# Stick-breaking attention summed by parts, in a hand-made pipeline of pieces

## The chip, the cores and the metric

The kernel runs on one core of a Trainium2 chip. The metric is the device time of one execution in microseconds (us), as the median of several runs; lower is better. The core has five engines with instruction queues of their own: TensorE (PE; its weight loads are listed as PEld), VectorE (DVE), ScalarE (ACT), GpSimd (POOL) and SyncE (SP), which here only issues DMAs. Each engine takes its own instructions strictly in the order in which they were laid down.

## The reference, cut to what matters

Two transformer layers on a sequence of 2048 positions and 1024 channels. The change touches one of three mixers of the second layer, the stick-breaking attention, which has 4 heads of 64 channels:

```
z       = q k^T / 8                       (128 queries at a time, all keys up to them)
log_1mb = where(mask, log_sigmoid(-z), 0)              (mask: key s < query t)
suffix  = cumsum(log_1mb, reverse) - log_1mb
a       = where(mask, exp(log_sigmoid(z) + suffix), 0)
out     = a v,  then an RMS norm for each head
```

Written without logarithms: let G[s] be the product of (1 - beta[j]) over all j from s to the end of the row. Then a[s] = G[s+1] - G[s], and out = sum over s of a[s] v[s]. The other mixers of this layer are a differential attention (4 heads, "diff") and a small windowed mean ("pool mixer").

## The kernel before, in words

Block 1, the whole first layer, takes the first part of the time and the feed-forward network the last; between them lies the attention stage (`block2`), from about 960 to 1975 us. It runs six units one after the other, in the order stick, diff, diff, stick, diff, diff. A stick unit holds two heads (r = 0 and 1). Each unit starts with four GEMM blocks of 512 positions (`unit_gemm`, its inner function `gemm`), which make keys, values and queries as pairs of float16 numbers (a high part and the remainder, the "low part"), and then goes over 16 rows of 128 queries; row i has (i + 1) * 128 keys. Up to four GEMM blocks are emitted ahead of the rows that use them. Tiles of keys, values and queries come from the pool U of 11 buffers, of which a unit takes 8.

A stick row (`stick`) is worked for each head in pieces of at most 1024 keys (PIECE), from the last keys to the first:

- `scores` makes z in PSUM for the whole row (lines 832, 833, 835), on TensorE.
- ScalarE writes sigmoid(-z) = 1 - beta into the tile g (line 973); one more column behind it holds 1.0 (a GpSimd memset, line 968) or the value carried from the piece before (VectorE copies, lines 970 and 980).
- VectorE's scan multiplies from right to left (line 975): g now holds G.
- GpSimd subtracts neighbours, A[s] = G[s+1] - G[s] (line 981).
- `parts` splits A into float16 halves: ScalarE casts the high part (line 845) and an engine that the caller names, VectorE for stick, subtracts to get the low part (line 846). A DMA transposes both (line 848).
- `spread` multiplies the transposed pieces with the values and adds them into PSUM (lines 869 and 870), when all pieces of the row and head are there.

A diff row uses `parts` and `spread` too, with GpSimd for the low part. The tiles g and A, and the two of a diff row, come from one pool E of 10 buffers (a piece of up to 512 keys takes one buffer for both).

The order of instructions on each engine is not that of the Python code: a list scheduler replays the program on a model of the chip and emits what is ready, earlier code first. So TensorE's GEMM matmuls of the next unit fill gaps between the pieces of the one that runs.

Of the kernel before, what the change touches and what calls it, by code (L numbers as in the profile page):

```python
# [7 lines left out]
F32 = mybir.dt.float32  # L8
# [31 lines left out]
PON = 2  # L40
EN = 10
UN = 11
LAST_B = 2
UNITS = (0, 2, 3, 1, 4, 5)
MIX_ROWS = (0, 2)
# [21 lines left out]
class Kernel:  # L67
# [638 lines left out]
    def block2(self):  # L706
        self.y2d = self.y_scratch("y2d")
        with ExitStack() as c2:
            self.ep = self.pool("E", EN, ctx=c2)
# [4 lines left out]
            self.sm = self.pool("asm", 4, ctx=c2)  # L714
            self.pg = self.pool("pg", PGN, PSUM, ctx=c2)
            self.sc = self.pool("sc", SCN, PSUM, ctx=c2)
# [4 lines left out]
            units = [units[j] for j in UNITS]  # L721
            self.turn = self.turn2 = 0
            self.later = []
            for u, (kind, k, *w) in enumerate(units):
                ops, gemm = self.unit_gemm(w)
                done = 0
# [20 lines left out]

    def etile(self):
        return self.ep.tile([128, PIECE + 8], F32, tag="e", name="e")

# [30 lines left out]

    def unit_gemm(self, cols):

# [3 lines left out]
        ks = [self.up.tile([128, S], F16, tag="u", name=f"k{r}") for r in range(2)]  # L787
        vs = [self.up.tile([128, NT // 2, 2, 128], F16, tag="u", name="v") for _ in range(2)]
        qs = []

        def gemm(b):
# [10 lines left out]
            ps = self.gemm_ct(wv, b)  # L802
            vt = self.one.tile([128, 2, 512], F16, tag="vt", name="vt")
            nc.scalar.copy(vt[:, 0], ps)
            nc.vector.tensor_tensor(vt[:, 1], ps, vt[:, 0], ALU.subtract)
            for x in range(2):
                nc.sync.dma_start_transpose(vs[b // 2][:, b % 2 * 4:b % 2 * 4 + 4, x], vt[:, x])
            ps = self.gemm_ct(wq, b)
# [8 lines left out]

        return (qs, ks, vs), gemm

    def scores(self, ops, r, i, strict):  # L820

        nc = self.nc
        qs, ks, _ = ops
        q = qs[i // 4][:, r, :, i % 4 * 128:(i % 4 + 1) * 128]
        W = (i + 1) * 128
        out = []
        for p in range(0, W, 512):
# [23 lines left out]
    def etiles(self, n):  # L851

        if self.last_rows:
            self.turn += 1
            e = self.tp.tile([128, 2, PIECE], F32, tag=("th", "tl")[self.turn % 2], name="e")
            return e[:, 0], e[:, 1]
        if n <= PIECE // 2:
            e = self.etile()
            return e[:, 0:PIECE // 2 + 8], e[:, PIECE // 2 + 8:]
        return self.etile(), self.etile()  # L860

    def spread(self, pieces, ops, cols, po):

# [3 lines left out]
        for x, (t, j, k) in enumerate(todo):  # L867
            v = ops[2][k // 8][:, k % 8, :, cols]
            nc.tensor.matmul(po, t[:, 0, j], v, start=x == 0, stop=False)  # L869
            nc.tensor.matmul(po[:, 0], t[:, 1, j], v[:, 0], start=False, stop=x == len(todo) - 1)  # L870

# [8 lines left out]
    def diff(self, ops, k, b):  # L880
# [3 lines left out]
        for c in range(4):  # L884
            po = self.po.tile([128, 2, 128], F32, tag="po", name="po")
            i = b * 4 + c
            W = (i + 1) * 128
            E = [(self.etiles(n), n) for n in (min(PIECE, W - p) for p in range(0, W, PIECE))]
            ss = self.sm.tile([128, 2, 4], F32, tag="ss", name="ss")
# [24 lines left out]
            for x, ((e1, e2), n) in enumerate(E):  # L914
                nc.vector.scalar_tensor_tensor(e1[:, 0:n], e2[:, 0:n], cf, e1[:, 0:n], ALU.mult, ALU.add)
                eng = nc.gpsimd if (i + x) % 4 < LO_POOL else nc.vector
                pieces.append((self.parts(e1, e2, n, eng), x * (PIECE // 128), n // 128))
            self.spread(pieces, ops, slice(0, 128), po)
# [32 lines left out]
    def stick(self, ops, k, b):  # L951

        nc = self.nc
        o8 = self.m.tile([128, 4, 2, 128], F32, tag="o4", name="o8")
        for c in range(4):
            po = self.po.tile([128, 2, 128], F32, tag="po", name="po")
            i = b * 4 + c
            W = (i + 1) * 128  # L960
            for r in range(2):
                sc = self.scores(ops, r, i, True)
                pieces, carry = [], None
                for p0 in reversed(range(0, W, PIECE)):
                    n = min(PIECE, W - p0)
# [5 lines left out]
                    for ps, p, w in sc:  # L971
                        if p0 <= p < p0 + PIECE:
                            nc.scalar.activation(g[:, p - p0:p - p0 + w], ps[:, 0:w], AF.Sigmoid, scale=-1.0)
                    rev = g[:, 0:n + 1][:, ::-1]
# [3 lines left out]
                    if p0:  # L978
                        carry = self.sm.tile([128, 1], F32, tag="carry", name="carry")
                        nc.vector.tensor_copy(carry, g[:, 0:1])  # L980
# [3 lines left out]
            nc.vector.tensor_copy(o8[:, c], po)  # L984
            yield

        o4 = self.summed(o8)

        def done():
            self.head_norm(o4, 64)  # L990
            self.finish(o4, k, b, self.col("sg"))

        self.later.append((LAST_DELAY if self.last_unit else DELAY, done))

# [356 lines left out]
```

## Time and profile before

| what | value |
|---|---|
| median of 3 runs | 3413.29 us (3409.84 to 3413.64) |
| profiled execution, its own time | 3417.88 us |
| span of the profiled execution | 3416.1 us |
| TensorE busy over the span | 3110.3 us (91%) |
| VectorE busy | 2274.2 us (67%) |
| ScalarE busy | 1217.8 us (36%) |
| GpSimd busy | 1357.9 us (40%) |
| mean granted TensorE clock | 0.969 of full speed |

The span is what the rows of the trace add up to; the time of the execution is 1.8 us longer, and lies 4.6 us above the median of the three runs. Busy shares are means over stages with different limits, so the stages have to be read apart.

### The profile page before, as it was taken

How to read it: one execution, taken by the hardware profiler on the slowest of the kernel's cores; microseconds unless marked ns; L12 is line 12 of the kernel's file. 1: busy time of each engine (PE TensorE's matmuls, PEld its weight loads, DVE VectorE, ACT ScalarE, POOL GpSimd, SP SyncE). 2: the span in 40 equal slices, each digit the busy share in tenths (PEclk: the TensorE clock that was granted, in tenths of full speed). 3: DMA queues.
4: the chain of work that ended last, by engine and by line, in shares of the span. 5: the costliest groups of instructions: out<-in, count | busy, mean ns of one | idle time of the engine just before them, and what ended most of it. 6: DMA issues, size and time to landing. Idle time of an engine off the chain costs nothing. (4 is left out here: it accounts for less than half of the span.)

```text
span 3416.1 us, 46957 instructions
## 1 busy us (share of the span) xinstructions
PE 3110.3 (91%) x17736; PEld 1576.9 (46%) x17736; DVE 2274.2 (67%) x3661; ACT 1217.8 (36%) x2291; POOL 1357.9 (40%) x1197
## 2 busy tenths in 40 slices
PE   8999998999988789958779898899999999989998
PEld 4454454785434445534335443344444444434443
DVE  6986979525638888879895744465655656754427
ACT  5223232322124466744564632233222332311103
POOL 5344344403335544565562511332322233244324
PEclk9999999999999899989999999899999999999999
DMA  5102021216756666646645788422222222453324
GB/s 189 38 17 47 13 50 44 58 44 176 179 140 125 125 127 134 134 96 125 127 91 106 154 214 195 117 69 80 80 84 68 74 90 81 161 190 134 110 98 168
DMA packets 597891, 371.85 MB, mean 109 GB/s; under 512 B 500640, under 2 KB 541344, under 8 KB 596640
## 3 DMA queue, kind: packets, MB, share of 16 engines
q1 hardware_dynamic: 590144, 348.22, 40.2%
q10 hardware_dynamic: 7520, 20.63, 1.8%
q8 instruction: 139, 2.28, 0.3%
q14 instruction: 88, 0.72, 0.1%
HBM read 162.70 MB, written 82.31 MB: 72 GB/s over the span
## 5 line engine op out<-in xcount | busy, mean ns | idle before, releaser
L144 PE MATMUL pg<-th,w 128*128 128x512 f16 x1344 | 520.2, 388 | 34.1 <-DVE r L592 11.6
L146 PE MATMUL pg<-th,w 128*128 128x512 f16 x1344 | 518.4, 386 | 7.2 <-POOL w L123 4.0
L145 PE MATMUL pg<-tl,w 128*128 128x512 f16 x1344 | 520.3, 387 | 0.7 <-DVE tl L183 0.7
L869 PE MATMUL po<-v,e 128*128 128x128 f16 (+1 forms) x1088 | 161.4, 252 | 98.6 <-DMA e<-e 85.3
L981 POOL TENSOR_TENSOR e<-e 128x128 f32<-128x128 f32 (+7 forms) x96 | 165.8, 1729 | 196.4 <-DVE e L975 145.8
L845 ACT CAST e<-e 128x1024 f16<-128x1024 f32 (+7 forms) x192 | 150.2, 794 | 224.6 <-POOL e L968 107.0
L846 POOL TENSOR_TENSOR e<-e 128x1024 f16<-128x1024 f32 (+4 forms) x96 | 157.5, 1655 | 180.3 <-ACT e L845 168.2
L145 PEld LDWEIGHTS <-w 128*128 128x128 f16 x1344 | 133.8, 100 | 175.3 <-issue 35.4
L144 PEld LDWEIGHTS <-w 128*128 128x128 f16 x1344 | 133.9, 100 | 171.6 <-issue 16.0
L146 PEld LDWEIGHTS <-w 128*128 128x128 f16 x1344 | 133.7, 100 | 165.8 <-issue 13.5
L975 DVE TENSOR_TENSOR_SCAN e<-e,few 128x129 f32<-128x129 f32 (+7 forms) x96 | 181.5, 1894 | 39.8 <-POOL e L968 31.0
L1075 POOL TENSOR_TENSOR w<-ws,w 128x1024 f16<-128x1024 f32 x20 | 48.6, 2431 | 393.0 <-ACT w L1074 393.0
L1107 PEld LDWEIGHTS <-w 128*128 128x128 f16 x1232 | 121.1, 98 | 172.9 <-issue 32.9
L832 PE MATMUL sc<-k,q 128*128 128x512 f16 (+2 forms) x480 | 174.1, 364 | 28.9 <-DVE e L895 23.7
L1106 PEld LDWEIGHTS <-w 128*128 128x128 f16 x1232 | 121.1, 98 | 165.5 <-ACT w L1074 18.7
L467 DVE SCALAR_TENSOR_TENSOR acc<-h,cols,acc 128x512 f32<-128x512 f32 x240 | 193.4, 826 | 2.4
L900 ACT ACTIVATE e<-e,nm 128x1024 f32<-128x1024 f32 (+4 forms) x192 | 171.1, 892 | 59.7 <-DVE e L895 39.1
L1108 PEld LDWEIGHTS <-w 128*128 128x128 f16 x1232 | 121.1, 98 | 150.0 <-issue 3.5
L833 PE MATMUL sc<-k,q 128*128 128x512 f16 (+2 forms) x480 | 171.7, 365 | 0.0
L869 PEld LDWEIGHTS <-e 128*128 128x128 f16 x1088 | 104.7, 101 | 126.5 <-issue 61.7
L123 POOL TENSOR_TENSOR w<-ws,w 128x1024 f16<-128x1024 f32 x52 | 120.2, 2313 | 96.1 <-ACT w L122 94.2
L870 PE MATMUL po<-v,e 128*128 128x64 f16 (+1 forms) x1088 | 155.3, 211 | 0.0
(318 smaller groups left out, 8018.1 us busy)
## 6 DMA issues: line engine op xcount, KB each, us to landing
mid<-md SPq DMA_DIRECT2D x88, 448.0 KB, 4.1
ws<-in_w SPq DMA_DIRECT2D x48, 512.0 KB, 3.9
md<-mid SPq DMA_DIRECT2D x44, 512.0 KB, 3.4
md<-mid SPq DMA_DIRECT2D x22, 768.0 KB, 5.0
q<-qn SPq DMA_DIRECT2D x96, 128.0 KB, 2.4
ws<-in_wg SPq DMA_DIRECT2D x22, 512.0 KB, 3.5
ws<-in_wu SPq DMA_DIRECT2D x22, 512.0 KB, 4.1
ws<-in_wd SPq DMA_DIRECT2D x22, 512.0 KB, 4.1
```

The costliest lines, as they stand in the source:

```text
L144: nc.tensor.matmul(ps, wh[:, k], th[:, k], start=k == 0, stop=False)
L145: nc.tensor.matmul(ps, wh[:, k], tl[:, k], start=False, stop=False)
L146: nc.tensor.matmul(ps, wl[:, k], th[:, k], start=False, stop=k == KD - 1)
L467: nc.vector.scalar_tensor_tensor(acc[:, ct], src, wcol, acc[:, ct], ALU.mult, ALU.add)
L832: nc.tensor.matmul(ps[:, 0:n], q[:, 0], kk, start=True, stop=False)
L833: nc.tensor.matmul(ps[:, 0:n], q[:, 1], kk, start=False, stop=not last)
L846: eng.tensor_tensor(fv[:, n:2 * n], A[:, 0:n], fv[:, 0:n], ALU.subtract)
L869: nc.tensor.matmul(po, t[:, 0, j], v, start=x == 0, stop=False)
L870: nc.tensor.matmul(po[:, 0], t[:, 1, j], v[:, 0], start=False, stop=x == len(todo) - 1)
L900: nc.scalar.activation(e[r][:, 0:n], e[r][:, 0:n], AF.Exp, bias=nm[:, len(sc) - 1:len(sc)], scale=-1.0, accum_out=ss[:, r, x:x + 1])
L975: nc.vector.tensor_tensor_scan(rev, rev, self.zero.to_broadcast([128, n + 1]), 1.0, ALU.mult, ALU.add)
L981: nc.gpsimd.tensor_tensor(A[:, 0:n], g[:, 1:n + 1], g[:, 0:n], ALU.subtract)
```

## The change

The sum over keys is rearranged. With a[s] = G[s+1] - G[s], the sum of a[s] v[s] over the keys below m is the sum of G[s] (v[s-1] - v[s]) over them, with v[-1] = 0, plus the boundary term G[m] v[m-1]. So for every key tile except the row's own (the last 128 keys, where the mask lies) the kernel now multiplies G itself with differences of the values, and the neighbours' subtraction over those keys is gone. For the own tile it still takes differences of G, 127 columns on VectorE into a small tile d; the free last column of d carries the boundary term, and the values of that tile (`vd`) have the last value of the tile before in that place.

- `unit_gemm` of a stick unit makes both sets of values in `v_steps`: a ScalarE copy out of PSUM, a GpSimd subtraction of 512 columns, two calls of `to_keys` (cast, low part on VectorE, two DMA transposes) where there was one, and about four GpSimd operations on single columns. It takes 10 U buffers instead of 8; the pool has 12 instead of 11.
- The scan starts from the carried column itself or from 1.0; the memset and the two carry copies are gone.
- The low part over the keys outside the own tile moves from VectorE to GpSimd. The cast and the low part of the own tile are instructions of their own, the latter on VectorE.
- The rows are cut into steps by hand: each piece is one step (scores of that piece alone, sigmoid, scan, own differences); its `split` (cast, low part, transpose) is emitted one step later and its matmuls three steps after that. The casts are pinned behind all that was emitted before them on ScalarE. The pieces run on over row ends and are flushed at the end of a unit.
- The pool E is split in two, of 6 and of 4 buffers: in a stick unit g takes one of the first and the float16 halves one of the second; a diff piece takes one of each, whatever its length.

```diff
-EN = 10
-UN = 11
+EN = (6, 4)
+UN = 12
+PIPE = 2
...
+        def v_steps(ps, b):
+            vf = self.one.tile([128, 528], F32, tag="m0", name="vf")
+            dv = self.one.tile([128, 528], F32, tag="m1", name="dv")[:, 0:512]
+            ends = self.sm.tile([128, 4], F32, tag="ends", name="ends")
+            nc.scalar.copy(vf[:, 1:513], ps)
...
+                nc.gpsimd.tensor_copy(vf[:, 0:1], vlast)
+            nc.gpsimd.tensor_tensor(dv, vf[:, 0:512], vf[:, 1:513], ALU.subtract)
+            to_keys(dv, b, vs)
+            if b < NB - 1:
+                nc.gpsimd.tensor_copy(vlast, vf[:, 512:513])
+            nc.gpsimd.tensor_copy(ends, vf[:, 0:512].rearrange("p (c t) -> p c t", t=128)[:, :, 0])
+            nc.gpsimd.tensor_copy(vf[:, 8:520].rearrange("p (c t) -> p c t", t=128)[:, :, 120], ends)
+            to_keys(vf[:, 1:513], b, vd)
...
-    def parts(self, A, free, n, eng):
+    def parts(self, srcs, A, free, n, eng, pin=False):
         nc = self.nc
         fv = free.bitcast(F16)[:, 0:2 * n]
-        nc.scalar.copy(fv[:, 0:n], A[:, 0:n])
-        eng.tensor_tensor(fv[:, n:2 * n], A[:, 0:n], fv[:, 0:n], ALU.subtract)
+        for src, o, w in srcs:
+            cast = nc.scalar.copy(fv[:, o:o + w], src)
+            if pin:
+                self.tc.keep_in_program_order(cast)
+            (nc.vector if w == 128 else eng).tensor_tensor(fv[:, n + o:n + o + w], src, fv[:, o:o + w], ALU.subtract)
...
+        def piece(i, r, p0, n, carry):
+            g = self.etile(0)
+            for ps, p, w in reversed(self.scores(ops, r, i, True, p0, p0 + n)):
+                nc.scalar.activation(g[:, p - p0:p - p0 + w], ps[:, 0:w], AF.Sigmoid, scale=-1.0)
+            rev = g[:, 0:n][:, ::-1]
+            nc.vector.tensor_tensor_scan(
+                rev, rev, self.zero.to_broadcast([128, n]), 1.0 if carry is None else carry, ALU.mult, ALU.add
+            )
+            srcs = [(g[:, 0:n], 0, n)]
+            if carry is None:
+                d = self.dp.tile([128, 128], F32, tag="d", name="d")
+                m = n - 128
+                nc.vector.tensor_copy(d[:, 127:128], g[:, m:m + 1])
+                nc.vector.tensor_tensor(d[:, 0:127], g[:, m + 1:n], g[:, m:n - 1], ALU.subtract)
+                srcs = [(d, m, 128)] + ([(g[:, 0:m], 0, m)] if m else [])
+
+            def split():
+                t = self.parts(srcs, g, self.etile(1), n, nc.gpsimd, True)
+                self.pipe.append((PIPE, lambda: sum_up(t)))
...
+            self.pipe.append((1, split))
+            return g[:, 0:1] if p0 else None
...
-                    g, A = self.etiles(n)
-                    if carry is None:
-                        nc.gpsimd.memset(g[:, n:n + 1], 1.0)
-                    else:
-                        nc.vector.tensor_copy(g[:, n:n + 1], carry)
...
-                    nc.vector.tensor_tensor_scan(
-                        rev, rev, self.zero.to_broadcast([128, n + 1]), 1.0, ALU.mult, ALU.add
-                    )
...
-                    nc.gpsimd.tensor_tensor(A[:, 0:n], g[:, 1:n + 1], g[:, 0:n], ALU.subtract)
-                    pieces.append((self.parts(A, g, n, nc.vector), p0 // 128, n // 128))
-                self.spread(pieces, ops, slice(r * 64, (r + 1) * 64), po[:, :, r * 64:(r + 1) * 64])
...
+                for p0 in reversed(range(0, W, PIECE)):
+                    carry = piece(i, r, p0, min(PIECE, W - p0), carry)
+                    self.step()
             yield
+        if b == NB - 1:
+            while self.pipe:
+                self.step()
+
+    def step(self):
+        self.pipe = [(n - 1, f) for n, f in self.pipe]
+        now = [f for n, f in self.pipe if n < 0]
+        self.pipe = [x for x in self.pipe if x[0] >= 0]
+        for f in now:
+            f()
```

## Rows read from the trace of the kernel before

**Rows 1.** Engine busy time in stretches of the attention stage (instructions in brackets).

```profile
core 0: us, PE busy (x) PEld busy (x) DVE busy (x) ACT busy (x) POOL busy (x), PEclk, DMA share, GB/s
1004.00:1222.00 218.00, 179.00 (x1199) 92.95 (x1197) 176.25 (x164) 96.21 (x202) 110.54 (x85) 0.91 0.62 122
1222.00:1458.00 236.00, 225.49 (x1472) 127.89 (x1472) 193.63 (x533) 168.62 (x381) 110.13 (x82) 0.99 0.67 134
1458.00:1678.00 220.00, 156.53 (x1091) 84.12 (x1092) 189.38 (x181) 99.57 (x215) 125.80 (x107) 0.88 0.59 112
1678.00:1975.00 297.00, 243.53 (x1518) 133.22 (x1517) 217.66 (x547) 172.99 (x384) 150.13 (x107) 0.97 0.59 124
...
1004.00:1030.00 26.00, 26.00 (x132) 12.37 (x131) 6.54 (x10) 7.02 (x14) 5.41 (x5) 1.00 0.37 86
```

**Rows 2.** Timeline of VectorE in the second stick unit: start, duration, instruction.

```profile
1584.29 1.21 DVE L975 TENSOR_TENSOR_SCAN e<-e,few 128x513 f32<-128x513 f32 x1
...
1585.79 1.90 DVE L846 TENSOR_TENSOR e<-e 128x1024 f16<-128x1024 f32 x1
1587.62 2.28 DVE L975 TENSOR_TENSOR_SCAN e<-e,few 128x1025 f32<-128x1025 f32 x1
1589.82 0.66 DVE L797 TENSOR_TENSOR kl<-pg,kh 128x512 f16<-128x512 f32 x1
1590.40 2.06 DVE L846 TENSOR_TENSOR e<-e 128x512 f16<-128x512 f32 x1
1592.39 1.21 DVE L975 TENSOR_TENSOR_SCAN e<-e,few 128x513 f32<-128x513 f32 x1
...
1601.81 1.20 DVE L846 TENSOR_TENSOR e<-e 128x1024 f16<-128x1024 f32 x1
```

**Rows 3.** Timeline of GpSimd in the same stretch.

```profile
1585.58 1.04 POOL L981 TENSOR_TENSOR e<-e 128x512 f32<-128x512 f32 x1 [1.92 <-DVE e L975]
1590.03 1.89 POOL L981 TENSOR_TENSOR e<-e 128x1024 f32<-128x1024 f32 x1 [3.42 <-issue]
```

**Rows 4.** Timelines of both at the start of the first stick unit.

```profile
1004.06 0.43 DVE L975 TENSOR_TENSOR_SCAN e<-e,few 128x129 f32<-128x129 f32 x1 [0.97 <-ACT e L973]
1005.32 0.29 DVE L846 TENSOR_TENSOR e<-e 128x128 f16<-128x128 f32 x1 [0.84 <-ACT e L845]
...
1004.57 0.40 POOL L981 TENSOR_TENSOR e<-e 128x128 f32<-128x128 f32 x1 [24.17 <-DVE e L975]
1019.10 2.13 POOL L123 TENSOR_TENSOR w<-ws,w 128x1024 f16<-128x1024 f32 x1 [14.14 <-ACT w L122]
```

**Rows 5.** Groups by line, whole span: busy, mean ns, idle before, releasers.

```profile
L981 POOL TENSOR_TENSOR e<-e 128x128 f32<-128x128 f32 (+7 forms) x96 | 165.8, 1729 | 196.4 <-DVE e L975 145.8 <-issue 16.2 <-PE sc L835 13.2
L846 DVE TENSOR_TENSOR e<-e 128x128 f16<-128x128 f32 (+7 forms) x96 | 132.7, 1388 | 9.7 <-ACT e L845 9.7
```

**Rows 6.** Groups by line and shape, 1000 to 1700 us.

```profile
L968 POOL MEMSET e<- 128x1 f32 x55 | 5.1, 96 | 7.7 <-DMA e<-e 7.7
L845 ACT CAST e<-e 128x128 f16<-128x128 f32 x13 | 3.7, 294 | 8.4 <-POOL e L981 7.5 <-DVE e L915 0.9
L1004 POOL COPY u<-last 128x16 f32<-128x16 f32 x5 | 2.4, 472 | 7.6 <-DMA q<-qn 4.5 <-DVE win L1019 1.8 <-DVE win L1022 1.3
```

**Rows 7.** Timelines of VectorE, SyncE, ScalarE over a diff row; landing of line 848's DMAs.

```profile
1389.49 0.69 DVE L895 TENSOR_SCALAR_CACHE_REDUCE e<-sc 128x512 f32<-128x512 f32 x1
...
1394.89 0.68 DVE L895 TENSOR_SCALAR_CACHE_REDUCE e<-sc 128x512 f32<-128x512 f32 x1
...
1401.65 1.81 DVE L915 SCALAR_TENSOR_TENSOR e<-e,cf 128x1024 f32<-128x1024 f32 x2
1410.29 1.95 DVE L915 SCALAR_TENSOR_TENSOR e<-e,cf 128x1024 f32<-128x1024 f32 x2
...
1406.31 4.37 SPq L848 DMA_TRANSPOSE e<-e  x2
...
1415.09 0.35 ACT L919 COPY o<-po 128x256 f32<-128x256 f32 x1
...
DMA to landing us min/median/max: 2.3/4.0/6.9
```

More of the change, by code (lines that the diff above doesn't have):

```diff
@@ L708, in block2 @@
         with ExitStack() as c2:
-            self.ep = self.pool("E", EN, ctx=c2)
+            self.ep = [self.pool(f"E{j}", n, ctx=c2) for j, n in enumerate(EN)]
             self.up = self.pool("U", UN, ctx=c2)
@@ L788, in unit_gemm, with to_keys @@
         vs = [self.up.tile([128, NT // 2, 2, 128], F16, tag="u", name="v") for _ in range(2)]
+        vd = [self.up.tile([128, NT // 2, 2, 128], F16, tag="u", name="vd") for _ in range(2)] if steps else None
+        vlast = self.sm.tile([128, 1], F32, tag="vlast", name="vlast") if steps else None
         qs = []
+        def to_keys(src, b, to):
+            vt = self.one.tile([128, 2, 512], F16, tag="vt", name="vt")
+            nc.scalar.copy(vt[:, 0], src)
+            nc.vector.tensor_tensor(vt[:, 1], src, vt[:, 0], ALU.subtract)
+            for x in range(2):
+                nc.sync.dma_start_transpose(to[b // 2][:, b % 2 * 4:b % 2 * 4 + 4, x], vt[:, x])
+        def v_steps(ps, b):
[3 more added lines that the diff above has]
+            nc.scalar.copy(vf[:, 1:513], ps)
+            if b == 0:
+                nc.gpsimd.memset(vf[:, 0:1], 0.0)
+            else:
+                nc.gpsimd.tensor_copy(vf[:, 0:1], vlast)
[6 more added lines that the diff above has]
+            to_keys(vf[:, 1:513], b, vd)
         def gemm(b):
@@ L802, in gemm @@
             ps = self.gemm_ct(wv, b)
[L803 to L807, printed above, removed]
+            if steps:
+                v_steps(ps, b)
+            else:
+                to_keys(ps, b, vs)
             ps = self.gemm_ct(wq, b)
@@ L816, in gemm, with scores @@
             qs.append(qq)
-        return (qs, ks, vs), gemm
-    def scores(self, ops, r, i, strict):
+        return (qs, ks, vs, vd), gemm
+    def scores(self, ops, r, i, strict, p0=0, end=S):
         nc = self.nc
-        qs, ks, _ = ops
+        qs, ks = ops[:2]
         q = qs[i // 4][:, r, :, i % 4 * 128:(i % 4 + 1) * 128]
@@ L826, in scores @@
         out = []
-        for p in range(0, W, 512):
+        for p in range(p0, min(W, end), 512):
             n = min(512, W - p)
@@ L849, in parts, with spread @@
         return t
[L851 to L862, printed above, removed]
+    def spread(self, pieces, ops, cols, po, diag=None, first=True, last=True):
         nc = self.nc
@@ L867, in spread @@
         for x, (t, j, k) in enumerate(todo):
-            v = ops[2][k // 8][:, k % 8, :, cols]
-            nc.tensor.matmul(po, t[:, 0, j], v, start=x == 0, stop=False)
-            nc.tensor.matmul(po[:, 0], t[:, 1, j], v[:, 0], start=False, stop=x == len(todo) - 1)
+            v = ops[3 if k == diag else 2][k // 8][:, k % 8, :, cols]
+            nc.tensor.matmul(po, t[:, 0, j], v, start=first and x == 0, stop=False)
+            nc.tensor.matmul(po[:, 0], t[:, 1, j], v[:, 0], start=False, stop=last and x == len(todo) - 1)
     def finish(self, o4, k, b, g):
@@ L955, in stick, with sum_up, ended, done @@
         nc = self.nc
-        o8 = self.m.tile([128, 4, 2, 128], F32, tag="o4", name="o8")
+        rows = {}
+        def piece(i, r, p0, n, carry):
[16 more added lines that the diff above has]
+                self.pipe.append((PIPE, lambda: sum_up(t)))
+            def sum_up(t):
+                c = i % 4
+                if r == 0 and carry is None:
+                    rows[i] = self.po.tile([128, 2, 128], F32, tag="po", name="po")
+                    if c == 0:
+                        rows["o8"] = self.m.tile([128, 4, 2, 128], F32, tag="o4", name="o8")
+                cols = slice(r * 64, (r + 1) * 64)
+                self.spread(
+                    [(t, p0 // 128, n // 128)], ops, cols, rows[i][:, :, cols], i, carry is None, p0 == 0
+                )
+                if r == 1 and p0 == 0:
+                    nc.vector.tensor_copy(rows["o8"][:, c], rows[i])
+                    if c == 3:
+                        ended()
+            self.pipe.append((1, split))
+            return g[:, 0:1] if p0 else None
+        def ended():
+            o4 = self.summed(rows["o8"])
+            def done():
+                self.head_norm(o4, 64)
+                self.finish(o4, k, b, self.col("sg"))
+            self.later.append((LAST_DELAY if self.last_unit else DELAY, done))
         for c in range(4):
-            po = self.po.tile([128, 2, 128], F32, tag="po", name="po")
             i = b * 4 + c
```

37 lines of the change are left out of this document (15 added, 22 removed).

## The prediction

> **What bounds the kernel now.** I read the busy times by stretch first, then the timelines of VectorE and GpSimd side by side inside a stick unit, then the groups by line for counts.
>
> The stretches [rows 1] cut the attention stage into its units: the first stick unit, two diff units, the second stick unit, the last two diff units. In the first pair of diff units TensorE is busy 225.5 of 236 us: there it sets the pace and nothing done to other engines buys time. In the two stick stretches TensorE is busy 179.0 of 218 and 156.5 of 220 us, so 39 + 63.5 = 102.5 us stand idle, and its granted clock is 0.91 and 0.88: its full level lapses there, after those idle moments, where the first diff pair has 0.99. VectorE is busy 81% and 86%. That looks like a stage bound by VectorE alone.
>
> The timelines say something sharper. Take one head of a row of 1536 keys, from one scan of 512 keys to the next, 1584.29 to 1592.39 = 8.10 us [rows 2]. The low part of 1024 columns takes 1.90 us there, and 1.20 at another place [rows 2]; at 1585.79 it meets GpSimd's subtraction, which runs from 1585.58 to 1586.62 [rows 3], and it ends 1.07 us after that. The low part of 512 columns takes 2.06 us: GpSimd runs from 1590.03 to 1591.92, and the low part ends 0.54 us later. So an instruction of VectorE with two inputs in SBUF stands still while GpSimd subtracts. The eviction at 1589.82, whose input lies in PSUM, runs its 0.66 us beside GpSimd at once. The scans have two such inputs as well. Add what each does when it has the way free: scans 1.21 + 2.28, GpSimd 1.04 + 1.89, low parts 1.07 + 0.54, together 8.03 of the 8.10 us. In these stretches the two engines work like one, and it has no slack. TensorE's idle time is what is left over.
>
> **The change, part by part.** I price the shared work of the two engines, in instructions with the way free, as a line through a short and a long one. Per unit 16 rows, two heads, mean width 1088 columns: over both units 69,632 columns in 96 pieces (64 first, 32 second).
>
> Removed. GpSimd's subtraction: 0.40 us at 128 columns [rows 4], 1.89 at 1024 [rows 3], so 0.187 us + 1.663 ns a column: 96 x 0.187 + 69,632 x 1.663 ns = 134 us (recorded 165.8 [rows 5], with its waits inside). VectorE's low part: 0.29 at 128 [rows 4], 1.20 at 1024 [rows 2], so 0.16 + 1.016 ns a column: 15 + 71 = 86 us (recorded 132.7 [rows 5]; the other 47 is standing still). 64 memsets at 0.096 [rows 6]: 6 us, each queued behind a subtraction. Sum 226. The carry copies go (64), and 64 copies of one column into d come: nothing.
>
> Added. GpSimd's low part over all but the own tiles: 61,440 columns in 88 instructions. The nearest row is the same operation on weights, 1024 columns in 2.13 us [rows 4]; with the 0.187 us start that is 1.9 ns a column: 16.5 + 116.5 = 133 us. Own tiles on VectorE: 64 times a subtraction of 127 and a low part of 128 columns, 0.29 each [rows 4]: 37 us. Sum 170. Scans stay: 0.43 at 129 and 2.28 at 1025 columns [rows 2, 4]; one column less is nothing, and a first value from a column, which no row shows, I bound by 0 and the 0.1 us of a one-column instruction [rows 6], at most 3 us for 32 carried pieces; I take 0.
>
> Rows net: 170 - 226 = -56 us. On VectorE alone, counted as busy time, it looks like 37 - 133 = -96; but a microsecond that goes from VectorE to GpSimd frees nothing where they exclude each other, and the low part is even dearer there (2.13 against 1.20). What is gained is only that the neighbours' subtraction is now made for 8,128 columns instead of 69,632.
>
> The Trainium skill has both views. Its page "Perfetto Trace Analysis", section Identifying the Most-Contended Engine, takes the occupancy of VectorE as a fair measure of how close to the limit it is; by that the gain would go with the 96 us. Its page "SBUF — State Buffer", section Who interferes with whom, says that a VectorE instruction with two SBUF inputs contends with a GpSimd instruction that reads SBUF, and that the second to issue is blocked wholly; by that it goes with the 56. The 2.06 us low part agrees with the second.
>
> Values. `v_steps` runs eight times. On the shared way each adds a subtraction of 512 columns on GpSimd (1.04 [rows 3]), about four one-column operations (0.10 to 0.47 [rows 6]; I take 0.3, so 1.1), and two low parts that read SBUF (0.66 each by the line above, 1.3): 3.5 us, 28 in all. One more cast and copy on ScalarE, two more transposes on SP: ScalarE is busy 44% and 45% of the stick stretches [rows 1]. The first unit's four blocks fall into its start, where GpSimd is busy 5.4 of 26 us and TensorE, with GEMMs, all of it [rows 1]: covered. The second unit's are emitted ahead into the diff rows before it or into its own first rows. I charge 14; bounds 0 and 28.
>
> ScalarE: 56 pieces have a second cast, 0.29 each [rows 6] = 16 us in 438 at 45% busy: nothing, unless late (a rival below). PSUM, TensorE and the transposes of pieces: same counts.
>
> Buffers. A stick unit holds 10 of 12 tiles of U (before 8 of 11), so one query tile less can be made ahead at either end of the stick units: 24 matmuls at the 0.2 us of the start (132 in 26 us [rows 1]) = 5 us of filler lost, twice; bounds 0 and 10, I take 5. The pools E: in a long diff row the second head's tile is written from 1394.89, and its transposes are issued from 1406.31 and land 4.0 us later [rows 7]: held 15.4 us. Rows come every 8.64 us (1401.65, 1410.29 [rows 7]), and four buffers are two rows, 17.3 us: enough by 1.9. The first head's, written from 1389.49 and free when the sum has been copied out at 1415.09 [rows 7], need 25.6 of the 25.9 us that six buffers give. Charge 0.
>
> Sum: -56 + 14 + 5 = -37 us, from the profiled execution's 3417.9 to 3381; the median of the runs lies 4.6 us lower: 3376. The shared work turns into time one for one only where it fills the stretch as in the 8.10 us; the bounds give -56 to -18.
>
> One more rule of the Trainium skill: "GPSIMD Engine Reference", section 4.1, counts about twice VectorE's time for a two-input elementwise operation; 2.13 to 1.20 is 1.8. By it the moved low part would cost some 15 us more, an estimate from that page, and the sum would be -22.
>
> **The rivals.** *VectorE alone was the bound.* Then its busy time, down by 96 and up by some 11 for `v_steps`, takes 85 us out of the stick stretches, inside the 102.5 us that TensorE idles there: 3328. For it: 81% and 86% busy, and pieces that no longer wait for one another within a row. Against: the 8.03 of 8.10 us. 0.17.
>
> *The pinned casts give the gain back.* A cast now stands behind the next piece's sigmoids, and they behind that piece's scores, which wait in TensorE's queue behind GEMM filler; GpSimd's low part, the transpose and all of SP's queue behind it wait for the cast. At 0.35 us a step, 96 steps lose 34 us: -3, no change, 3410. For it: each engine keeps its order. Against: the step of delay is about 4 us. 0.12.
>
> *Slower: the split pool holds up the diff rows.* In 24 rows with two pieces (the last eight of a unit, but for the last unit, whose later rows use other tiles) the second heads' buffers allow one row per half a hold. The slack is 1.9 us. If the hold grows from 15.4 to 23 us, a row takes 11.5 instead of 8.64 and 24 rows lose 69: +32, 3445. It decides against the change from a loss of 44 us, 1.8 us a row, a hold of 21. For it: first heads' tiles have 0.3 us to spare, and short rows lose their shared buffer. Against: no buffer is taken away, and 6 to 4 is nearly the proportion of the holds. 0.13.
>
> **How the numbers follow.** The forecast has 0.58. Half of the first rival and all of the third outside the range leave 0.78 inside it: 3330 to 3412. This kernel's runs tell a change from none at about 0.2%, 7 us: faster 0.77 (the forecast, the first rival, a little of the second), same 0.10, slower 0.13.
>
> **What the new profile would show.** GpSimd's subtraction gone from the pieces, its low parts at 2.1 to 2.4 us per 1024 columns; VectorE's own-tile instructions at two or three times 0.29 us, where they meet them. The stick stretches together about 40 us shorter, TensorE's idle time there near 65, its clock a few hundredths higher; the diff pairs as long as before. I am wrong if the stick stretches shrink by 80 us (the way was not the bound), if ScalarE's casts wait for sigmoids and GpSimd for casts, or if diff rows come later than every 9 us with waits on tile releases.

## The result: 0.5% slower

The changed kernel takes 3430.14 us (3426.54 to 3434.86, four runs) against 3412.10 us for the kernel before on the same chip; the ratio is 1.0053, with an interval of 1.0038 to 1.0068. The forecast was 3376 us. The profiled execution of the changed kernel took 3431.76 us, with a span of 3430.0 and a mean granted clock of 0.961 (before 0.969).

The same stretches as in [rows 1], in the changed kernel (busy us of each engine, granted clock in the third column from the end):

```profile
1004.00:1222.00 218.00, 172.77 (x1237) 93.85 (x1233) 183.10 (x241) 114.31 (x281) 121.66 (x70) 0.93 0.69 135
1222.00:1458.00 236.00, 227.77 (x1442) 127.31 (x1442) 191.99 (x499) 163.52 (x351) 107.59 (x85) 0.99 0.63 126
1458.00:1678.00 220.00, 147.06 (x1020) 78.97 (x1021) 176.34 (x189) 94.91 (x230) 124.60 (x72) 0.79 0.58 116
1678.00:1975.00 297.00, 256.58 (x1498) 136.47 (x1496) 214.20 (x549) 176.67 (x386) 138.28 (x101) 0.95 0.53 113
```

TensorE is busier in the diff stretches than in [rows 1] and less busy in both stick stretches, and in the second its granted clock fell from 0.88 to 0.79. The units have moved, so from here on they are cut at their own marks: a stick unit from its first scan to its last copy of a row's sum. First the changed kernel by these marks, all instructions:

```profile
1006.20:1209.50 203.30, 160.03 (x1164) 87.41 (x1162) 173.96 (x214) 102.84 (x247) 113.01 (x61) 0.92 0.68 133
1209.50:1449.90 240.40, 232.59 (x1458) 129.01 (x1456) 195.38 (x509) 164.81 (x370) 114.53 (x90) 0.99 0.63 127
1449.90:1679.90 230.00, 154.68 (x1092) 83.93 (x1091) 182.83 (x209) 103.54 (x244) 124.94 (x72) 0.80 0.59 117
1679.90:1985.30 305.40, 262.87 (x1550) 141.00 (x1549) 213.47 (x548) 176.51 (x387) 140.73 (x102) 0.95 0.55 117
```

Then only what touches the PSUM tile of the GEMM blocks (the PE column is the GEMM filler and counts it), in the changed kernel:

```profile
1006.20:1209.50 203.30, 96.08 (x390) 10.14 (x15) 9.42 (x16) 0.92 0.68 133
1209.50:1449.90 240.40, 139.78 (x586) 13.00 (x19) 13.24 (x23) 0.99 0.63 127
1449.90:1679.90 230.00, 72.50 (x271) 6.00 (x9) 7.57 (x13) 0.80 0.59 117
1679.90:1985.30 305.40, 111.56 (x477) 11.03 (x16) 11.64 (x20) 0.95 0.55 117
```

and in the kernel before:

```profile
1004.10:1238.80 234.70, 126.86 (x528) 14.25 (x21) 12.37 (x21) 0.92 0.62 123
1238.80:1455.40 216.60, 114.48 (x472) 13.58 (x20) 11.44 (x20) 0.98 0.67 133
1455.40:1690.00 234.60, 90.20 (x383) 8.02 (x12) 9.43 (x16) 0.89 0.61 116
1690.00:1973.00 283.00, 83.14 (x362) 8.26 (x12) 9.32 (x16) 0.97 0.58 120
```

Put together from such windows, with idle as length less TensorE's busy time:

| kernel | two stick units: us | GEMM matmuls (busy us) | TensorE idle | two diff stretches: us | GEMM matmuls (busy us) | TensorE idle | span |
|---|---|---|---|---|---|---|---|
| before | 469.3 | 911 (217.1) | 106.5 | 499.6 | 834 (197.6) | 60.0 | 3416.1 |
| changed | 433.3 | 661 (168.6) | 118.6 | 545.8 | 1063 (251.3) | 50.3 | 3430.0 |
| before, split E (e13) | 486.0 | 872 (209.3) | 118.3 | 513.0 | 871 (210.7) | 57.0 | 3437.7 |
| changed, one pool E (e14) | 394.4 | 617 (152.1) | 95.8 | 551.3 | 1107 (257.9) | 49.7 | 3392.4 |
| best (e11) | 377.5 | 698 (166.5) | 71.9 | 525.8 | 1023 (243.0) | 45.4 | 3357.1 |

The stick units did become 36.0 us shorter. But they hold 250 GEMM matmuls less, 48.5 us of them, and TensorE idles 12.1 us more. The diff stretches took in 229 more (53.7 us), of which their gaps hid little: TensorE's idle time there fell by 9.7 us (the first had only 8.3 us of it, the second 51.6), and they are 46.2 us longer. Over the whole span TensorE's idle time is 305.8 us before (3416.1 - 3110.3) and 306.4 after (3430.0 - 3123.6): the change bought none of it. Its busy time, for the same 17,736 matmuls, grew by 13.3 us while its mean clock fell, and that is the 13.9 us of the span. As a span is busy time plus idle time, this says where the time went and not yet why.

VectorE in the changed kernel, in the first stick unit:

```profile
1090.18 0.68 DVE L808 TENSOR_TENSOR vt<-pg,vt 128x512 f16<-128x512 f32 x1
...
1107.54 3.88 DVE L997 TENSOR_TENSOR_SCAN e<-e,few 128x1024 f32<-128x1024 f32 x2
1111.35 2.15 DVE L890 TENSOR_TENSOR e<-d,e 128x128 f16<-128x128 f32 x1
...
1113.81 0.27 DVE L1005 TENSOR_TENSOR d<-e 128x127 f32<-128x127 f32 x1
...
1117.13 1.21 DVE L997 TENSOR_TENSOR_SCAN e<-e,few 128x512 f32<-128x512 f32 x1
...
1118.45 1.96 DVE L1005 TENSOR_TENSOR d<-e 128x127 f32<-128x127 f32 x1
```

and GpSimd there:

```profile
1090.04 2.21 POOL L890 TENSOR_TENSOR e<-e 128x1024 f16<-128x1024 f32 x1
...
1111.08 2.27 POOL L890 TENSOR_TENSOR e<-e 128x1024 f16<-128x1024 f32 x1 [0.74 <-ACT e L887]
...
1117.55 2.71 POOL L890 TENSOR_TENSOR e<-e 128x1024 f16<-128x1024 f32 x1 [0.49 <-ACT e L887]
```

An own-tile low part of 128 columns, 0.29 us with the way free [rows 4], takes 2.15: it stands until GpSimd ends at 1113.35. The subtraction of 127 columns takes 0.27 in a gap of GpSimd and 1.96 beside it. The eviction at 1090.18, with one input in PSUM, is not slowed: it takes 0.68 us while GpSimd runs from 1090.04 to 1092.25. All 128 of the own-tile instructions, and the pinned casts, by line (busy, mean ns, idle before and releaser):

```profile
L890 DVE TENSOR_TENSOR e<-d,e 128x128 f16<-128x128 f32 x64 | 52.8, 826 | 3.4 <-ACT e L887 3.1 <-issue 0.2
L1005 DVE TENSOR_TENSOR d<-e 128x127 f32<-128x127 f32 x64 | 39.3, 615 | 0.0
L887 ACT CAST e<-d 128x128 f16<-128x128 f32 x64 | 19.0, 297 | 108.4 <-DVE d L1005 61.5 <-issue 21.9 <-POOL e L890 16.4
```

Together 92.1 us of VectorE, where the forecast priced 37 of work; the other 55 is standing still. ScalarE's casts stand 61.5 us behind that subtraction.

VectorE's combining instruction of long diff rows in the second diff unit, which answers to [rows 7], for the same first and last of six rows (it takes 0.13 us more from row to row in both kernels, where nothing holds it up, so the rows can be told apart). Before:

```profile
1393.29 1.68 DVE L915 SCALAR_TENSOR_TENSOR e<-e,cf 128x1024 f32<-128x1024 f32 x2
...
1446.53 2.35 DVE L915 SCALAR_TENSOR_TENSOR e<-e,cf 128x1024 f32<-128x1024 f32 x2
```

and after:

```profile
1386.05 1.68 DVE L948 SCALAR_TENSOR_TENSOR e<-e,cf 128x1024 f32<-128x1024 f32 x2
...
1439.53 2.35 DVE L948 SCALAR_TENSOR_TENSOR e<-e,cf 128x1024 f32<-128x1024 f32 x2
```

The rows come every 10.65 us before (53.24 / 5) and every 10.70 after (53.48 / 5), though TensorE runs 586 GEMM matmuls in this diff stretch in place of 472. The 8.64 us of [rows 7] was one gap, and one of the shortest. In the last diff stretch the same five gaps take 57.8 us in place of 48.2; with one shared pool (e14 below) they take 57.4, so there it is not the split that delays them.

### The profile page after: what moved, and what is told of

It is laid out like the page before. It is cut to its first block, busy times and chain, and to the rows that moved or that the text cites. A ratio compares the mean times of both kernels' runs of the same rounds, so it can differ in the third digit from the quotient of the medians.

```text
span 3430.0 us, 47081 instructions
## 1 busy us (share of the span) xinstructions
PE 3123.6 (91%) x17736; PEld 1583.5 (46%) x17736; DVE 2256.0 (66%) x3717; ACT 1231.4 (36%) x2363; POOL 1359.3 (40%) x1147
## 5 line engine op out<-in xcount | busy, mean ns | idle before, releaser
L890 POOL TENSOR_TENSOR e<-e 128x1024 f16<-128x1024 f32 (+6 forms) x168 | 314.2, 1880 | 305.8 <-ACT e L887 272.1
L902 PE MATMUL po<-v,e 128*128 128x256 f16 (+1 forms) x1024 | 157.9, 257 | 89.1 <-DMA e<-e 77.3
L997 DVE TENSOR_TENSOR_SCAN e<-e,few 128x128 f32<-128x128 f32 (+7 forms) x96 | 204.7, 2145 | 24.1 <-ACT e L995 22.0
L147 PEld LDWEIGHTS <-w 128*128 128x128 f16 x1344 | 134.1, 100 | 165.4 <-issue 16.7
L872 PE MATMUL sc<-k,q 128*128 128x512 f16 (+2 forms) x480 | 173.6, 364 | 37.7 <-ACT e L995 25.2
L933 ACT ACTIVATE e<-e,nm 128x1024 f32<-128x1024 f32 (+4 forms) x192 | 171.1, 892 | 57.8 <-DVE e L928 44.8
L887 ACT CAST e<-e 128x1024 f16<-128x1024 f32 (+7 forms) x184 | 141.9, 783 | 100.8 <-DVE e L948 47.8
L902 PEld LDWEIGHTS <-e 128*128 128x128 f16 x1088 | 106.5, 102 | 116.5 <-DMA e<-e 56.0
L903 PE MATMUL po<-v,e 128*128 128x128 f16 (+1 forms) x1024 | 151.7, 214 | 0.0
L928 DVE TENSOR_SCALAR_CACHE_REDUCE e<-sc,nm 128x512 f32<-128x512 f32 (+3 forms) x192 | 122.7, 646 | 27.8 <-PE sc L873 15.2
```

Source lines behind the costliest of these rows:

```text
L147: nc.tensor.matmul(ps, wl[:, k], th[:, k], start=False, stop=k == KD - 1)
L887: cast = nc.scalar.copy(fv[:, o:o + w], src)
L890: (nc.vector if w == 128 else eng).tensor_tensor(fv[:, n + o:n + o + w], src, fv[:, o:o + w], ALU.subtract)
L902: nc.tensor.matmul(po, t[:, 0, j], v, start=first and x == 0, stop=False)
L933: nc.scalar.activation(e[r][:, 0:n], e[r][:, 0:n], AF.Exp, bias=nm[:, len(sc) - 1:len(sc)], scale=-1.0, accum_out=ss[:, r, x:x + 1])
L997: nc.vector.tensor_tensor_scan(rev, rev, self.zero.to_broadcast([128, n]), 1.0 if carry is None else carry, ALU.mult, ALU.add)
```

## The experiments

Each run is compared with the kernel before on the same chip; "against the changed kernel" is the difference of the two ratios to it, times 3413 us, uncertain by some 7 us. The rivals tried are: the shared way of VectorE and GpSimd, VectorE alone, pinned casts, the split pool, `v_steps`, and filler.

**e1: casts not pinned.**

```diff
-                t = self.parts(srcs, g, self.etile(1), n, nc.gpsimd, True)
+                t = self.parts(srcs, g, self.etile(1), n, nc.gpsimd)
```

> The changed kernel with the casts no longer pinned. The trace of the changed kernel shows ScalarE's casts waiting 61 us in the two stick units for VectorE's own-tile differences, with the sigmoids queued behind them and TensorE's scores waiting 25 us for the sigmoids. Theory C (coupling: the pins make ScalarE, and through it TensorE, wait): the scores' wait falls to some 5 us and the time to 3405 to 3418. Theory F (filler: shorter stick units only hold fewer GEMM matmuls of the next unit, TensorE's idle time over the whole stage does not fall, so the end does not move): no more than 7 us from 3430.

3414.99 us, ratio 0.9996 [0.9987, 1.0005]: 19 us less than the changed kernel. But the scores' wait for the sigmoids, expected to fall from 25.2 to some 5 us, rose to 32.5, and the casts stand as long as before behind the own tile's subtraction (61.2 us against 61.5). What the pins cost, and how, stays unclear; one other candidate stands at e16 to e18.

**e2: plain values, `v_steps` and the two tiles `vd` left out** (the sums then use the values in place of their differences).

```diff
-            if steps:
-                v_steps(ps, b)
-            else:
-                to_keys(ps, b, vs)
+            to_keys(ps, b, vs)
...
-            v = ops[3 if k == diag else 2][k // 8][:, k % 8, :, cols]
+            v = ops[2][k // 8][:, k % 8, :, cols]
```

> The changed kernel without the second set of values: the values are split once, as before, and used for all key tiles, so the sums are of G with the plain values (that part of the computation is left out), and a stick unit holds 8 of the 12 tiles of U, not 10. Theory V (the value work and the two tiles it holds are the loss): 3385 to 3410, with the GEMM blocks of the next unit back inside the stick units. Theory C: 3420 to 3430. Theory F without V: within 7 us of 3430.

3401.47 us, 0.9956 [0.9944, 0.9969]: 33 us less, more than the upper bound of 28 put on `v_steps`.

**e3: low part back on VectorE**, all else as changed.

```diff
-                t = self.parts(srcs, g, self.etile(1), n, nc.gpsimd, True)
+                t = self.parts(srcs, g, self.etile(1), n, nc.vector, True)
```

> The changed kernel with all low parts of the stick pieces on VectorE, as before the change. Free of waits this takes 88 x 0.16 us + 61,440 x 1.016 ns = 76 us on VectorE for the 133 us on GpSimd, so 57 us less on the way that the two engines share. If that way set the end: about 3375. Theory F: the stick units end earlier still, and the time stays within 10 us of 3430. Theory C: the low part waits for the cast on VectorE too and holds up the next scan behind it: 3430 to 3450.

3364.14 us, 0.9851 [0.9837, 0.9864]: 69 us less than the changed kernel. GpSimd loses 133 us of work by the forecast's prices and VectorE gains 76 (88 x 0.16 us + 61,440 x 1.016 ns): the shared way predicts 57 less, and VectorE alone predicts 76 more. (VectorE's recorded busy time fell, from 2256.0 to 2237.8 us, as the standing still went with the work on GpSimd.) VectorE's timeline of this run:

```profile
1111.80 0.27 DVE L890 TENSOR_TENSOR e<-d,e 128x128 f16<-128x128 f32 x1
...
1112.52 0.28 DVE L1005 TENSOR_TENSOR d<-e 128x127 f32<-128x127 f32 x1
1112.71 1.22 DVE L890 TENSOR_TENSOR e<-e 128x1024 f16<-128x1024 f32 x1
1113.85 0.68 DVE L808 TENSOR_TENSOR vt<-pg,vt 128x512 f16<-128x512 f32 x1
1114.45 2.34 DVE L997 TENSOR_TENSOR_SCAN e<-e,few 128x1024 f32<-128x1024 f32 x1
```

Every instruction here has, to 0.06 us, the time that [rows 2, 4] show with the way free.

**e4: the kernel before with U of 10 buffers** (`UN = 11` becomes 10).

> The kernel before with 10 tiles of U instead of 11, so that beside a stick unit 2 are free for the next unit's GEMMs, as in the changed kernel. If the number of free tiles decides how much filler the stick units hold: 8 to 20 us slower than before, 3420 to 3432. If not: within 7 us of 3412.

3419.29 us, 1.0009 [1.0000, 1.0018]: a U buffer is worth some 3 us, hardly clear of noise. The filler in the two stick units fell by 116 matmuls, to 795, and the time hardly moved: filler that leaves them need not cost its own length.

**e5: low part on VectorE and casts not pinned.**

```diff
-                t = self.parts(srcs, g, self.etile(1), n, nc.gpsimd, True)
+                t = self.parts(srcs, g, self.etile(1), n, nc.vector)
```

> The changed kernel with the low parts of the stick pieces on VectorE and the casts not pinned. If the pins' 15 us and the engine's 66 us add: 3349. If the pins only hurt because ScalarE waited for a VectorE that GpSimd held up (nobody holds it up now): 3360 to 3368.

3366.15 us, 0.9859 [0.9845, 0.9872], the same as e3: with the low part on VectorE the pins cost nothing.

**e6: no pipeline, no pins.** Each piece's split and sum follow at once.

```diff
-                t = self.parts(srcs, g, self.etile(1), n, nc.gpsimd, True)
-                self.pipe.append((PIPE, lambda: sum_up(t)))
+                t = self.parts(srcs, g, self.etile(1), n, nc.gpsimd)
+                sum_up(t)
...
-            self.pipe.append((1, split))
+            split()
```

> The changed kernel without the hand-made pipeline: split and matmuls of a piece are emitted right behind its scan and no cast is pinned; the list scheduler alone spreads them. Theory F with the pipeline as the cause of the lost filler: the first stick unit holds over 480 GEMM matmuls (changed kernel 388, unpinned 374, before 526), and the time is 3385 to 3405. If the arithmetic itself is the cause (shorter rows in the scheduler's model leave less to fill): under 430 GEMM matmuls, and 3405 to 3430.

3462.45 us, 1.0145 [1.0129, 1.0160]. The filler is back in the stick units (933 matmuls), and they are longer by 88 us, the run by 31. Against e1, which has no pins either, the run is 51 us longer and holds 933 such matmuls in place of 615: the hand-made pipeline pays, and it is what moved the filler out. Giving the U tiles back (e2) brought only 696.

**e7: the kernel before with the low part on GpSimd.**

```diff
-                    pieces.append((self.parts(A, g, n, nc.vector), p0 // 128, n // 128))
+                    pieces.append((self.parts(A, g, n, nc.gpsimd), p0 // 128, n // 128))
```

> The kernel before with the low part of the stick pieces on GpSimd. With the way that VectorE and GpSimd share, this adds 96 x 0.187 + 69,632 x 1.9 ns - 86 = 64 us to the stick units: they grow by 50 to 70 us and the kernel by 30 to 70 (some of it filled with GEMMs). By VectorE's busy time alone (the other view), VectorE is relieved of 133 us and the time falls, to under 3400.

3473.33 us, 1.0172 [1.0158, 1.0186]: 58 us slower. With VectorE alone as the bound it would have been faster.

**e8: as e2, with the two tiles `vd` held** (filled with zeros once in a unit, and read for the own tile, whose values the sums so leave out).

```diff
+            if steps and b == 0:
+                for t in vd:
+                    nc.gpsimd.memset(t, 0.0)
             to_keys(ps, b, vs)
```

> As the run without the second set of values (3401 us), but the two U tiles are allocated, set to zero once in a unit and read for the own tile, so that a unit holds 10 tiles again (the values of own tiles are left out of the sums). If the tiles cost the 29 us: about 3430. If the operations on the values do: about 3401.

3405.92 us, 0.9972 [0.9963, 0.9981]: of e2's 33 us the buffers are about 5, less than the uncertainty and with the zero filling inside (7.1 us of GpSimd in all), and the operations of `v_steps` some 28.

**e9 and e10: less filler, in the kernel before and in the changed one.** The first matmul of each GEMM block after the first unit keeps its place in program order.

```diff
-            nc.tensor.matmul(ps, wh[:, k], th[:, k], start=k == 0, stop=False)
+            mm = nc.tensor.matmul(ps, wh[:, k], th[:, k], start=k == 0, stop=False)
+            if k == 0 and getattr(self, "hold", False):
+                self.tc.keep_in_program_order(mm)
...
+                        self.hold = u > 0
                         gemm(done)
+                        self.hold = False
```

> The kernel before, in which no unit's GEMM matmuls may be laid out ahead of what was emitted before them on TensorE, so that the stick units hold no GEMMs of the next unit. TensorE then idles through the stick units. Slower by 100 us or more, 3500 to 3650; it is the partner of the next run.

> The changed kernel with the same hold on the GEMMs. Theory F (the change did shorten the stick rows by some 36 us, and lost it because 253 GEMM matmuls that had filled TensorE's gaps there moved into the diff units): without filler on either side the change shows its gain, and this run is 30 us or more faster than the run before it, though the changed kernel is 18 us slower than the kernel before. If the rows themselves are no faster, or the diff units lose time for another reason (the split pool E): no faster than it, or slower by about 18 us.

3661.12 us (1.0717 [1.0701, 1.0733]) and 3635.74 us (1.0642 [1.0626, 1.0658]): here the change makes the kernel 25 us faster. Filler did not vanish: 413 and 295 matmuls stay in the stick units. So with less GEMM work laid into the stick units the change pays; but since the diff stretches lengthen here too, by 35 us, while they take in 94 matmuls more, these two runs do not separate the displaced filler from other causes.

**e11: low part on VectorE, pipeline one step shorter** (e3 and `PIPE = 1`).

> The changed kernel with the low parts on VectorE (3364 us) and the matmuls of a piece emitted two steps after its split, not three. The layout has 332 and 273 GEMM matmuls between the first and the last sum of the two stick units, where three steps have 326 and 274. Theory F: the same filler, so within 7 us of 3364.

3359.52 us, 0.9832 [0.9817, 0.9847]. This is the best version, 1.7% faster than before and 75 us faster than the changed kernel.

**e12: as e11 with pools of five and five** (`EN = (5, 5)`).

> As the run before it with the pool E split 5 and 5. The layout now has 390 and 324 GEMM matmuls in the stick units, 109 more, 24 us of TensorE at 0.22 us. Theory F, filler as the lever: 3340 to 3358. If the fifth buffer of G, taken away, is what counts: slower than 3364, by the waits for tiles.

3387.07 us, 0.9913 [0.9897, 0.9930]. More filler in the stick units (811 matmuls against 698) and still slower by 28 us: TensorE then idles 26.1 us in the first diff pair, against 12.0 in e11. So filler kept in the stick units is not a gain in itself.

**e13: the kernel before with the split pool**, six and four, one of each for a piece.

```diff
-EN = 10
+EN = (6, 4)
...
-        if n <= PIECE // 2:
-            e = self.etile()
-            return e[:, 0:PIECE // 2 + 8], e[:, PIECE // 2 + 8:]
-        return self.etile(), self.etile()
+        return self.etile(0), self.etile(1)
```

> The kernel before with its ten shared score buffers split into six large and four small ones, one of each per piece, and nothing else. If the split is what lengthens the diff units (the third rival), they lengthen here too, by 20 to 36 us together, and the run lands at 3430 to 3450 us. If the displaced filler is the cause, the split costs little: within 7 us of the kernel before, with the diff units within 5 us of 217 and 283 us.

3439.55 us, 1.0072 [1.0059, 1.0085]: the split, with the shared buffer of short pieces gone (which e14 does not bring back), costs the kernel before 25 us. Its waits from 1004 to 1700 us (us in total, times, longest):

```profile
ACT e L970 <- DMA e<-e: 94.3, 39, 5.2
ACT e L845 <- POOL e L978: 44.4, 29, 3.5
ACT e L845 <- POOL e L965: 9.3, 5, 3.6
```

```profile
PE po L866 <- DMA e<-e: 103.0, 49, 11.1
```

Line 970 is the sigmoid, 866 the sum, 845 the cast, 965 the memset and 978 the neighbours' subtraction. The same in the kernel before, where these lines but the cast stand three further on:

```profile
ACT e L973 <- DMA e<-e: 5.9, 3, 2.8
ACT e L845 <- POOL e L981: 69.7, 37, 4.6
ACT e L845 <- POOL e L968: 107.0, 43, 5.3
```

```profile
PE po L869 <- DMA e<-e: 66.3, 39, 5.4
```

The sigmoids stand 94.3 us in place of 5.9 behind transposes that still hold a buffer. ScalarE as a whole does not wait longer for it: its casts (line 845) wait 53.7 us for GpSimd in place of 176.7. What tells of a loss is TensorE's wait of the sums for their transposes, 103.0 us in place of 66.3.

By the table above 16.7 of the longer time lie in the stick units and 13.4 in the diff stretches.

**e14: the changed kernel with one pool of ten.**

```diff
-EN = (6, 4)
+EN = 10
...
-            self.ep = [self.pool(f"E{j}", n, ctx=c2) for j, n in enumerate(EN)]
+            self.ep = [self.pool("E", EN, ctx=c2)] * 2
```

> The changed kernel with one shared pool of ten score buffers in place of six and four. If the split costs the diff units 20 to 36 us, this run is that much faster than the changed kernel: 3394 to 3410 us. If the displaced filler is the cause, it stays within 7 us of the changed kernel's 3430 us.

3394.24 us, 0.9938 [0.9925, 0.9952]: 39 us less than the changed kernel and faster than before. The gain lies in the stick units, 433.3 to 394.4 us; the diff stretches, where the third rival had put the loss, are not shorter. The waits do not say how: from 1004 to 1700 us ScalarE waits 14.5 us for tiles of the pool to be released here, and 16.5 in the changed kernel.

**e15: the best version with one pool of ten** (e11 with the edit of e14).

> The best version so far (low part on VectorE, one piece in the pipeline, 3359.5 us) with one shared pool of ten score buffers. If the split costs, 3330 to 3345 us; if not, within 7 us of 3359.5 us.

3378.35 us, 0.9887 [0.9873, 0.9902]: 19 us slower than e11. With the low part on VectorE and the pipeline a step shorter, the split is the better one; the loss lies in the last diff stretch, 313.5 us against 291.2.

**e16 to e18: which pool runs short.** Five and five; then six and five, and seven and four, each at the price of one U buffer (`UN = 11`).

> The changed kernel with five large and five small score buffers in place of six and four. If the small pool runs short (the halves wait for transposes to land), this gives back most of the 36 us that one shared pool gave: 3392 to 3408 us. If the large pool runs short (sigmoids wait for the matmuls of a piece six before), five are worse than six: above 3440 us. If only the sharing counts, the time stays near 3430 us.

> The changed kernel with six large and five small score buffers, one U buffer given up for it (which by an earlier run costs some 3 us). Small pool short: 3390 to 3410 us. Large pool short: within 7 us of 3430 us.

> The changed kernel with seven large and four small score buffers, one U buffer given up for it. Large pool short: 3390 to 3410 us. Small pool short: within 7 us of 3430 us.

3415.10 us (0.9997 [0.9988, 1.0007]), 3433.54 (1.0055 [1.0040, 1.0070]) and 3417.10 (1.0008 [0.9998, 1.0017]): 19 less, the same, and 15 less than the changed kernel. None of them gives the 39 us of the shared pool, and no one reading fits all three: five large ones are not worse than six, yet seven are better. The small pool alone is not what runs short. One other difference stands out, TensorE's waits before the matmuls of the windowed mean (line 1090). In the changed kernel:

```profile
PE pm L1090 <- POOL hn L189: 13.0, 1, 13.0
...
PE pm L1090 <- DVE win L1086: 7.4, 2, 4.0
...
PE pm L1090 <- DVE win L1083: 4.6, 1, 4.6
```

These are 25.0 us; in e14, by the same view, 4.4 and 3.5:

```profile
PE pm L1090 <- DVE win L1083: 4.4, 1, 4.4
PE pm L1090 <- DVE win L1086: 3.5, 2, 2.1
```

So 17 of e14's 26.5 us less idle (306.4 to 279.9) lie at these few matmuls, which in the changed kernel are laid down at places in the order where their inputs are late. In e1 the same sum is 11.6 us, 13.4 less than in the changed kernel, and TensorE's idle time is 10.6 less (295.8): its gain, too, may be this order and not the pins as such. The sums are 22.5 us in e17 and 7.7 in e18, but also 19.2 before, 26.1 in e8 and 1.0 in e13.

## Why the prediction was wrong, point by point

- **VectorE and GpSimd share one way: right.** That VectorE stands still is shown by the instructions: 2.15 us beside GpSimd against 0.27 (e3). The page "SBUF — State Buffer" of the Trainium skill, section Who interferes with whom, says this of two SBUF inputs; the trace agrees with these two numbers. e3 moved the time by -69 us where the shared way said -57, and e7 by +58, both against the sign of the work put on VectorE or taken off it. By the occupancy rule of the Trainium skill's "Perfetto Trace Analysis", section Identifying the Most-Contended Engine, e7 should have gained: VectorE's busy time fell by 73 us, from 2274.2 to 2201.6. A low part also holds up its own piece longer on GpSimd (2.27 us against 1.22), and the two times do not separate this from the shared way. The -56 itself was not measured by a run of its own; what e3 shows is that the low part was moved to the wrong engine, and the forecast had that price (2.13 against 1.20) and used it.
- **The step that failed first: "Buffers ... Charge 0."** The split pool costs 39 us in the changed kernel (e14), and with one pool that kernel is faster than the kernel before; in the kernel before the split costs 25 (e13). The third rival named the cause and gave it 0.13, but looked for it in the diff rows alone, and its tell there did not come: in the second diff unit the rows come as often as before, and in the last stretch one pool does not bring them sooner. The forecast's 8.64 us a row was one short gap; at 10.65 four buffers outlast the hold of 15.4 us by 5.9, not by 1.9. The 39 us lie in the stick units, where no hold was worked out: a g from its sigmoid through split, transpose and three more steps, a pair of halves from the cast to the landing. In e13 the sigmoids' waits show such holds. In the changed kernel the waits do not, and whether the split costs there by holds or by the other order that the scheduler makes of it is not shown.
- **The second: "turns into time one for one".** The stick units fell by 36 us, almost the 37 of the forecast, and the run did not: TensorE's idle time there went from 106.5 to 118.6, where "near 65" was expected of 102.5 by the old marks, and its clock went down in the second one where "a few hundredths higher" was. 250 matmuls left them, 48.5 us, where the forecast had 24 twice, and the diff pairs, expected "as long as before", are 46 us longer. That a matmul that leaves costs its own time, as the forecast priced it, is not shown: e4 lost 116 for 3 us, e14 has 44 fewer than the changed kernel and is 39 us faster, and e6 and e12 have more and are slower than their partners.
- **`v_steps`, 14 us with bounds 0 and 28:** 28 by e8, at its upper bound: no gain from the cover assumed for half of it shows.
- **Pinned casts, 0:** 19 us (e1), and 0 when the low part is on VectorE (e5). The second rival gave 34 for casts that stand behind sigmoids; the waits of e1 do not bear that out, and what makes the 19 is open.
- **U, 5 us with the filler:** 3 (e4) to 5 (e8).
- **VectorE alone as the bound: wrong**, by e3 and e7.

The forecast of -37 and the measured +18 are 55 us apart. The pool (39 where 0 was charged), the pins (19 where 0 was) and `v_steps` (33 with its buffers, where 14 + 5 was) make 72: taken out one at a time they overlap, and e5 and e15 show two of them vanish or turn round with the low part on VectorE (e15 with a shorter pipeline too). That all of them lengthen how long a piece stays in the pipeline, and cost by that, is argued from those two runs, not shown.

Open is how much of e14's 39 us is the pool itself and how much the other order of TensorE's queue that came with it (the matmuls of line 1090), and the same of e1's 19 us. It was not tried to hold that order fixed.

## What to carry to other kernels

Where one engine's gaps are filled with later work in a fixed order, judge a change by that engine's idle time and clock over the whole span, and not by the length of the stage that was changed: here the stage got 36 us shorter, shed filler, and gave nothing back. When a pipeline keeps more pieces alive, work out the hold of every buffer in the stage that is pipelined, not only in its neighbours, and read the spacing of rows over many of them. When each edit lays the order of all engines anew, a difference of 10 to 20 us may be a few instructions laid down too early: look for them in the waits. And moving an instruction with two SBUF inputs from VectorE to GpSimd lengthened the sum of the two where they met (2.13 us against 1.20). Here the rearranged sum and the hand-made pipeline were good, and with the low part left on VectorE and the pipeline a step shorter they made 3359.5 us.

## What the runs showed of the hardware

- A short instruction of VectorE can stand as long as a long one of GpSimd runs: a low part of 128 columns took 2.15 us beside GpSimd's low part of 1024 columns, and 0.27 without (e3). The 128 short own-tile instructions stood 55 us in all.
- GpSimd stands still as well, behind what VectorE has under way. Its low part of 1024 columns took 2.13 us with VectorE idle ([rows 4]; VectorE runs nothing from 1018.80 to 1023.37 there), so the forecast's price had no waiting in it. The one at 1111.08 began 0.34 us before the scans ended (1107.54 + 3.88 = 1111.42) and took 2.27 us; the one at 1117.55 began 0.79 us before the scan ended (1117.13 + 1.21 = 1118.34) and took 2.71.
- TensorE's granted clock does not follow its idle time alone. In the second stick unit it was 0.80 with 75 us of idle time in the changed kernel and 0.89 with 49 in e11, but also 0.89 with 66 before and 0.81 with 64 in e13.
